# Attention in a bidirectional encoder layer: TensorE in a written order, with half of the values' projection, the queries and some of the next keys among the scores, and three steps from scores to transposes

## The chip, the core and the metric

The kernel runs on one core of one Trainium2 chip. The core has five engines, each with a queue of its own: TensorE (PE; its weight loads are listed as PEld), VectorE (DVE), ScalarE (ACT), GpSimd (POOL) and SyncE (SP), which issues most transfers. An engine takes its instructions in the order in which the built program has them, and semaphores make one wait for another. The metric is the device time of one execution in microseconds (us), lower is better; runs are compared on the same chip. The runs of the kernel before took 1503.9, 1504.07 and 1504.43 us.

## What is computed

One encoder layer on 1024 tokens and 16 meta tokens, width 1024: a combined projection, a neighbourhood attention, a gated recurrence in both directions, a gated sum of the two, an output projection and a feed-forward part, in float32. The change lies in the attention alone. The tokens are a grid of 16 rows by 64 columns; a token sees a window of 8 rows by 16 columns, and the meta tokens:

```python
# q,k,v: (B, N_META+T, H, dh), 8 heads of 64
s_win = einsum('brchd,brjwhd->bhrcjw', qg, k_blk) * scale
s_win = where(in_win, s_win + bias, -1e30)
s_meta = einsum('brchd,bmhd->bhrcm', qg, km) * scale
p = softmax(concatenate([s_win, s_meta]))
o_grid = einsum('bhrcjw,brjwhd->brchd', p_win, v_blk) + einsum('bhrcm,bmhd->brchd', p_meta, vm)
```

## The kernel before

Every float32 product is made from three matmuls of a split: each operand is a high part, which ACT casts (`hi`), and a low part, which DVE subtracts (`lo`); `mm3` (lines 122 to 124) does high by high, high by low and low by high. Below, a block is one call of `mm3`: three matmuls of the same width.

The attention runs in four pairs of heads (`NPAIR`, index `p`). A pair has three projections of 128 columns of weights over the tokens in `aT`: queries (`C_QN`, 16 blocks of 512 columns in two banks `mm`), keys (`C_KN`) and values (`C_VN`), each in three pieces of 8 blocks: 256 columns, 272 (the last 16 are the meta tokens) and 512. `proj_steps` makes them and, when it starts, splits the next weights (`load_block`: the cast L112 or L115 and the subtraction L113 or L116; those of queries, which are scaled, are L115 and L116). The order of weights is queries, keys, values, next queries.

The results go from the banks into tiles: queries into `QX` (a high half and a low half for each head of the pair), keys into `KS` (high) and `KL` (low), values into `vT`, which PE transposes (`vpt`, L831) and ACT and DVE split into `V`. There is one buffer of each, so the next pair's keys may be written when this pair's scores are done. `V` block 8 holds the meta values; it comes from the copy L825 of the 272 piece.

Then come 16 steps, one for each head `i` of the pair and strip `s` of 8 columns, in groups of four strips. `scores(s, i)` does two matmuls of 432 columns (288 at the grid's two edges) into one of two banks `s` (L848, L849); DVE adds mask and bias and takes the minimum (L854), ACT the exponential and its sum (L856), DVE the reciprocal and the scaling (L857, L858) into `pr`. `values(s, i)` transposes `pr` in three or four pieces into one of two banks `t` (`ppt`, L869, L871); ACT casts them into `PH` (L880), DVE subtracts into `PL` (L881), both named `PT` in the profile. After a group's fourth strip, the same function does the 12 matmuls with `V` into the bank `pov` (L885 to L894); DVE copies their low half (L896, `low`) and adds it into the pair's output `OT` (L898), which POOL writes out. A step's transposes stand two steps behind its scores:

```python
            for st in steps:
                pend.append((*st, *scores(*st)))
                if len(pend) > 2:
                    values(*pend.pop(0))
            for st in pend:
                values(*st)
```

Beside this, SP loads each pair's mask (`NB`) and bias, which POOL subtracts (L784), and POOL makes sums of `aT` for a later stage (`block_sums`, L189, L193).

What sets the order: inside `tc.manual_schedule(engines=...)`, the engines named run their instructions as the code is written. The context `in_order` names PE, ACT and DVE and is closed (`in_order.close()`) when the first pair's keys are done. From there a scheduler orders every engine when the program is built, from what depends on what and its own estimate of when it will be ready. It lays the next pair's projections, which the code has after the steps, between the steps; in the last pair it lays products of the next stage there (gates, L928 to L930).

Of the kernel before, what the change touches and what calls it, by code (L numbers as in the profile page):

```python
# [18 lines left out]
P = 128  # L19
# [3 lines left out]
TH = 512  # L23
# [25 lines left out]
def layer(ctx: ExitStack, tc: tile.TileContext, x, meta, w_in, w_na, w_hg, w_o, w_up, w_dn,  # L49
# [685 lines left out]
    def first_query():  # L735

        hi, lo = block_of(C_QN)
        early[C_KN] = block_of(C_KN)
        for h in range(2):
            ps = bank("mm", "mm").rearrange("p a b -> p (a b)")  # L740
            for k in range(KC):
                mm3(ps, hi[:, k], lo[:, k], *(t[:, k, :TH] for t in aT[h]), k == 0, k == KC - 1)
            yield ps
# [3 lines left out]
    query_ps = list(first_query())  # L747
# [9 lines left out]
    with (tc.tile_pool(name="npr", bufs=1, side="right", reuse_waits="tile") as npr,  # L757
# [17 lines left out]

        for p in range(NPAIR):
# [10 lines left out]
            def ev_q(ps, t0, n):  # L787
                for i in range(2):
                    act.copy(strips(QX[i], 64 * i, t0, n), grid(ps, 64 * i))
                for i in range(2):  # L790
                    b = 64 * i
                    dve.tensor_tensor(strips(QX[i], 64 - b, t0, n), grid(ps, b),
                                      strips(QX[i], b, t0, n).bitcast(F32), op=ALU.subtract)
            if p == 0:
                for h in range(2):
                    ev_q(query_ps[h], h * TH, TH)
            else:
                proj(C_QN + p * P, ev_q)

            def ev_k(ps, t0, n):  # L800
                for i in range(2):
                    act.copy(strips(KS[i], 64 * i, t0, n), grid(ps, 64 * i))
                for i in range(2):
                    b = 64 * i
                    dve.tensor_tensor(strips(KL[i], b, t0, n), grid(ps, b),
                                      strips(KS[i], b, t0, n).bitcast(F32), op=ALU.subtract)
                    act.copy(strips(KS[i], 64 - b, t0, n), strips(KS[i], b, t0, n).bitcast(F32))

            def mev_k(ps):
                for i in range(2):  # L810
                    b = 64 * i
                    m = ps[b:b + 64].unsqueeze(1).broadcast_to([64, 8, NM])
                    hi = KS[i][b:b + 64, :, P:]
                    act.copy(hi, m)
                    act.copy(KS[i][64 - b:128 - b, :, P:], m)
                    dve.tensor_tensor(KL[i][b:b + 64, :, P:], m, hi.bitcast(F32), op=ALU.subtract)
            proj(C_KN + p * P, ev_k, mev_k)
            in_order.close()

# [6 lines left out]
            proj(C_VN + p * P, ev_vn, mev_vn)  # L826
            for b in (0, 4, 8):
# [33 lines left out]
            def values(s, i, js, pr):  # L861
# [20 lines left out]
                if e < 3:  # L882
                    return
# [12 lines left out]
                dve.tensor_copy(low, ov[64:])  # L896
# [992 lines left out]
```

## Time and profile before

| | |
|---|---|
| profiled execution | 1503.19 us, its span 1501.4 us |
| runs of the kernel | 1503.9, 1504.07, 1504.43 us |
| PE | 9200 matmuls in the trace, 1488.8 us busy |
| granted TensorE clock | 0.999 of full speed |
| attention, first scores to last products | from 354.5 us of the span to about 562 us |
| one pair, from values' transposes to the next pair's | 57.27, 56.48, 56.44 us |

The profile is one execution, recorded by the hardware's profiler. A row of the timeline has an instruction's start in us from the span's start, how long it took, engine, line, operation, output and inputs by the program's names, partitions and elements, and the count where equal ones are merged; in brackets the idle time of the engine ahead of it and what ended it. Rows of groups have the sum of busy time and the mean in ns of one. A row of windows has the stretch, its length, then for each engine in the order PE, PEld, DVE, ACT, POOL the busy us and the count of instructions, then the clock, the busy share of the transfer engines and GB/s. PE's matmuls are pipelined and their ends modelled: a 512-column matmul is shown with 0.39 us and the next starts 0.23 later. So what a matmul takes is read from starts.

### The profile page before, as it was taken

What the parts mean: (1) busy time and instruction counts of PE and PEld (TensorE: products, weight loads), DVE (VectorE), ACT (ScalarE), POOL (GpSimd) and SP (SyncE); (2) the same over time, 40 slices, a digit from 0 to 9 for tenths busy, and PEclk for the clock granted to TensorE, in tenths of its full rate; (3) what the DMA queues carried; (4) which work ended last, traced back from release to release, by engine and by line L of the source; (5) the groups of instructions that cost most, each with busy time, mean ns of one, the idle gap of its engine ahead of it and who ended that gap; (6) DMA issues with size and microseconds to landing.
All of it is one profiled execution on the core that took longest, in us unless ns stands there. A gap on an engine that the chain in (4) does not pass through costs nothing.

```text
span 1501.4 us, 23486 instructions
## 1 busy us (share of the span) xinstructions
PE 1488.8 (99%) x9200; PEld 1249.0 (83%) x9200; DVE 1045.1 (70%) x1612; ACT 669.5 (45%) x1197; POOL 366.3 (24%) x346
## 2 busy tenths in 40 slices
PE   9999999999999999999999999999999999999998
PEld 8888888888888888888888887888888888888886
DVE  7867676756696696665485479777777445877876
ACT  7232323136565576343132355555555534334444
POOL 3313131314423400110000122234444200231242
PEclk9999999999999999999999999999999999999999
DMA  4211011112313237445655125444444677563224
GB/s 171 60 29 58 29 58 29 58 51 98 109 43 95 98 116 235 147 155 176 209 169 210 43 99 175 155 155 154 154 155 155 209 259 234 189 225 115 95 83 155
DMA packets 142592, 195.61 MB, mean 130 GB/s; under 512 B 8193, under 2 KB 90369, under 8 KB 142481
## 3 DMA queue, kind: packets, MB, share of 16 engines
q1 hardware_dynamic: 133216, 172.86, 35.2%
q10 hardware_dynamic: 7088, 13.91, 2.4%
q0 software_dynamic: 2176, 7.34, 1.3%
q8 instruction: 72, 1.18, 0.3%
q14 instruction: 40, 0.32, 0.1%
HBM read 139.56 MB, written 54.53 MB: 129 GB/s over the span
## 4 chain that ended last, share of the span: by engine, by line
PE 92%; DVE 5%; ACT 2%; issue 1%; DMA 0%; POOL 0%; ACTq 0%; POOLq 0%; DVEq 0%
PE mm L122 11%; PE mm L123 11%; PE mm L124 11%; PE mm L1564 5%; PE pa L1564 5%; PE pb L928 4%; PE pb L929 4%; PE pb L930 4%; PE pc L1564 4%; PE pb L1564 4%; PE pc L929 3%; PE pc L930 3%; PE pc L928 3%; PE pa L930 2%; PE pa L929 2%; PE pa L928 2%
## 5 line engine op out<-in xcount | busy, mean ns | idle before, releaser
L122 PE MATMUL mm<-aT,hi 128*128 128x512 f32 (+2 forms) x600 | 214.5, 358 | 0.0
L124 PE MATMUL mm<-aT,lo 128*128 128x512 f32 (+2 forms) x600 | 211.7, 353 | 0.0
L123 PE MATMUL mm<-aT,hi 128*128 128x512 f32 (+2 forms) x600 | 211.0, 352 | 0.0
L97 DVE TENSOR_TENSOR dl<-ur,dh 128x1024 fp32r<-128x1024 f32 x54 | 71.1, 1316 | 87.3 <-ACT dh L96 85.4
L96 ACT CAST dh<-ur 128x1024 fp32r<-128x1024 f32 x54 | 56.9, 1054 | 166.7 <-issue 91.1
L122 PEld LDWEIGHTS mm<-aT,hi 128*128 128x128 f32 x600 | 113.3, 189 | 12.5
L124 PEld LDWEIGHTS mm<-aT,lo 128*128 128x128 f32 x600 | 113.2, 189 | 12.5
L123 PEld LDWEIGHTS mm<-aT,hi 128*128 128x128 f32 x600 | 113.4, 189 | 11.4
L1352 ACT ACTIVATE uv<-uv 128x512 f32<-128x512 f32 x48 | 30.4, 633 | 79.3 <-DVE uv L1460 52.8
L112 ACT CAST hi<-raw 128x1024 fp32r<-128x1024 f32 x26 | 27.3, 1050 | 64.5 <-PE mm L123 62.1
L854 DVE CUSTOM_DVE_ANT_0 pr<-nsc,NB 128x432 f32<-128x432 f32 (+1 forms) x64 | 35.2, 558 | 30.0 <-issue 21.6
L1655 POOL TENSOR_TENSOR w<-w,tt 128x512 f32<-128x512 f32 x16 | 23.4, 1460 | 133.1 <-DVE tt L1654 112.3
L113 DVE TENSOR_TENSOR lo<-raw,hi 128x1024 fp32r<-128x1024 f32 x26 | 38.4, 1476 | 18.0 <-ACT hi L112 14.0
L303 POOL TENSOR_TENSOR Y<-X,TN 128x512 f32<-128x512 f32 x20 | 31.1, 1556 | 80.3 <-DVE X L300 80.3
L122 PE MATMUL mm<-wh,mT 128*128 128x512 f32 x128 | 50.2, 392 | 0.0
L123 PE MATMUL mm<-wl,mT 128*128 128x512 f32 x128 | 50.1, 391 | 0.0
L124 PE MATMUL mm<-o,lo 128*128 128x512 f32 x128 | 49.9, 390 | 0.1
L124 PE MATMUL mm<-wh,mT 128*128 128x512 f32 x128 | 49.9, 390 | 0.0
L123 PE MATMUL mm<-o,hi 128*128 128x512 f32 x128 | 49.8, 389 | 0.0
L122 PE MATMUL mm<-o,hi 128*128 128x512 f32 x128 | 49.8, 389 | 0.0
L1564 PE MATMUL mm<-dl,dh 128*128 128x512 f32 x124 | 48.6, 392 | 0.3 <-DVE dl L97 0.2
L1564 PE MATMUL mm<-dh,dl 128*128 128x512 f32 x124 | 48.3, 390 | 0.0
(459 smaller groups left out, 4439.3 us busy)
## 6 DMA issues: line engine op xcount, KB each, us to landing
raw<-in_w_in SPq DMA_DIRECT2D x56, 512.0 KB, 4.0
ur<-usp SPq DMA_DIRECT2D x54, 512.0 KB, 3.6
raw<-in_w_up SPq DMA_DIRECT2D x16, 1024.0 KB, 6.1
usp<-us SPq DMA_DIRECT2D x60, 256.0 KB, 2.3
sg<-gsp SPq DMA_DIRECT2D x16, 512.0 KB, 5.0
w<-in_w_dn SPq DMA_DIRECT2D x16, 512.0 KB, 4.8
usp<-uv SPq DMA_DIRECT2D x30, 256.0 KB, 2.4
gsp<-gv ACTq DMA_DIRECT2D x24, 256.0 KB, 2.4
```

The costliest lines, as they stand in the source:

```text
L96: act.copy(hi, src)
L97: dve.tensor_tensor(lo, src, hi.bitcast(F32), op=ALU.subtract)
L113: dve.tensor_tensor(lo[:, :kc], raw[:, :kc], hi[:, :kc].bitcast(F32), op=ALU.subtract)
L122: pe.matmul(ps, lh, rh, start=first, stop=False)
L123: pe.matmul(ps, lh, rl, start=False, stop=False)
L124: pe.matmul(ps, ll, rh, start=False, stop=last)
L303: pool.tensor_tensor(fap(Y, h, mid3), fap(X, h, mid3), fap(TT, 0, [[4, g], [n + 3, 2], [0, h]]), op=ALU.mult)
L854: dve.tensor_tensor_reduce(out=pr[:, :w], in0=sc[:, :w], in1=NB[:, i, o:o + w], scale=1.0, scalar=3.0e38, op0=ALU.add, op1=ALU.min, accum_ ...
L928: pe.matmul(ps, lhs[0][:, c], rhs[0][:, k], start=first and k == 0, stop=False, skip_group_check=True)
L929: pe.matmul(ps, lhs[0][:, c], rhs[1][:, k], start=False, stop=False, skip_group_check=True)
L930: pe.matmul(ps, lhs[1][:, c], rhs[0][:, k], start=False, stop=k == 3, skip_group_check=True)
L1564: pe.matmul(ps, a[n == 2][:, q, j * P:(j + 1) * P], b[n == 1][:, q], start=first and n == 0, stop=last and n == 2, skip_group_check=True)
```

## The change

- `in_order` is closed after a pair's keys as before, but opened again for PE alone. So PE runs as written until the seventh step of the last pair; ACT and DVE are left to the scheduler.
- The values' first 12 blocks (`VAHEAD`) are written ahead of the scores. The other 12, the transposes of the values, the next pair's queries and the first of its keys are one stream (`fills`), from which `columns` takes blocks into two gaps of each step, by a table of columns (`GAPS`).
- A step's transposes stand three steps behind its scores, and a group's products (`products`, cut out of `values`) in the step after.
- The last three transposes and the last products (`tail`) are written into the next pair's keys. The next pair's queries are evicted after steps 13 and 16, and evictions of keys are held back until the scores are done.
- The copy into `low` goes from DVE to ACT.

The lines of the kernel after are some 50 to 70 further down: L869 is L919, L848 is L898, L831 is L859, L825 is L854, L822 is L851, L856 is L906, L880 is L930, L885 is L937.

First, PE in the second pair, around its first scores and the transposes of its values. `nsc` are scores, `mm` with `aT_89` and `aT_90` the values' 512 piece (with `aT_87` and `aT_88` their smaller pieces or the next queries), `vpt` the values' transposes. Before, from the last matmul ahead of the values' first eight transposes to that of the meta values:

```order
L124 MATMUL mm<-aT_87,lo 128x512
L831 MATMUL vpt<-ident,vT 128x128 x8
L122 MATMUL mm<-aT_87,hi 128x512
L848 MATMUL nsc<-KS_4068,QX_4066 128x288
L849 MATMUL nsc<-KL_4070,QX_4066 128x288
L123 MATMUL mm<-aT_88,hi 128x512
L124 MATMUL mm<-aT_87,lo 128x512
L122 MATMUL mm<-aT_87,hi 128x512
L848 MATMUL nsc<-KS_4068,QX_4066 128x432
L849 MATMUL nsc<-KL_4070,QX_4066 128x432
L123 MATMUL mm<-aT_88,hi 128x512
L831 MATMUL vpt<-ident,vT 128x128
```

After, from the second scores:

```order
L898 MATMUL nsc<-KS_4067,QX_4065 128x432
L899 MATMUL nsc<-KL_4069,QX_4065 128x432
L122 MATMUL mm<-aT_87,hi 128x272
L123 MATMUL mm<-aT_88,hi 128x272
L124 MATMUL mm<-aT_87,lo 128x272
L122 MATMUL mm<-aT_87,hi 128x272
L123 MATMUL mm<-aT_88,hi 128x272
L124 MATMUL mm<-aT_87,lo 128x272
L859 MATMUL vpt<-ident,vT 128x128
L122 MATMUL mm<-aT_89,hi 128x512
L123 MATMUL mm<-aT_90,hi 128x512
L124 MATMUL mm<-aT_89,lo 128x512
```

All of the values' blocks stood ahead of the scores, and so of these rows; the matmuls between the scores are the next pair's queries. Now the scores lie among the values' blocks, and the transpose of the meta values comes right behind the blocks of 272 columns, the last of which makes them.

Second, ACT over the same stretch, up to the transposes' casts. `pr,sm` are exponentials, `hi` the cast of the next projection's weights, `vT` copies of the values (16 for the meta values, 64x8x64 for the 512 piece), `Vn` casts of the transposed values. Before:

```order
L822 COPY vT<-mm 64x8x32 x2
L825 COPY vT<-mm 128x16
L822 COPY vT<-mm 64x8x32 x2
L112 CAST hi<-raw 128x1024
L822 COPY vT<-mm 64x8x64 x2
L856 ACTIVATE pr,sm<-pr,mn 128x288
L856 ACTIVATE pr,sm<-pr,mn 128x432
L833 CAST Vn<-vpt 128x8x64 x2
L856 ACTIVATE pr,sm<-pr,mn 128x432 x2
L833 CAST Vn<-vpt 128x2x64
L880 CAST PT_5025<-ppt 128x3x128
```

After:

```order
L906 ACTIVATE pr,sm<-pr,mn 128x288
L906 ACTIVATE pr,sm<-pr,mn 128x432
L854 COPY vT<-mm 128x16
L851 COPY vT<-mm 64x8x32 x2
L861 CAST Vn<-vpt 128x2x64
L906 ACTIVATE pr,sm<-pr,mn 128x432 x2
L930 CAST PT_5013<-ppt 128x3x128
L930 CAST PT_5013<-ppt 128x4x128
L906 ACTIVATE pr,sm<-pr,mn 128x288
L112 CAST hi<-raw 128x1024
L906 ACTIVATE pr,sm<-pr,mn 128x432
L851 COPY vT<-mm 64x8x64 x2
```

The copies into `vT` stood ahead of the first exponential. Now that of the meta values stands behind two exponentials, and those of the 512 piece behind a cast of weights and one exponential more. (In the first pair the orders are others: there `vT` of 16 stands ahead of the second exponential, and the 512 piece's copies ahead of the cast.)

Third, PE where the other values are turned, from the second of two query blocks behind the values' last block:

```order
L122 MATMUL mm<-aT_87,hi 128x512
L123 MATMUL mm<-aT_88,hi 128x512
L124 MATMUL mm<-aT_87,lo 128x512
L898 MATMUL nsc<-KS_4068,QX_4066 128x432
L899 MATMUL nsc<-KL_4070,QX_4066 128x432
L859 MATMUL vpt<-ident,vT 128x128 x4
L919 MATMUL ppt<-ident,pr 128x128 x3
L921 MATMUL ppt<-ident,pr 128x128
L122 MATMUL mm<-aT_87,hi 128x512
```

Before, the eight transposes stood ahead of the fifth scores, as the first rows show; now four stand behind the seventh scores, with a step's transposes of `pr` right behind them.

The core of the diff:

```diff
+    query_ps = []
+    def query_steps(p, tile):
+        hi, lo = block_of(C_QN + p * P)
+        early[C_KN + p * P] = block_of(C_KN + p * P)
         for h in range(2):
-            ps = bank("mm", "mm").rearrange("p a b -> p (a b)")
+            ps = tile()
             for k in range(KC):
                 mm3(ps, hi[:, k], lo[:, k], *(t[:, k, :TH] for t in aT[h]), k == 0, k == KC - 1)
-            yield ps
+                if k == KC - 1:
+                    query_ps.append(ps)
+                yield TH
...
+        def ev_q(h, i):
+            b = 64 * i
+            ps = query_ps[h]
+            act.copy(strips(QX[i], b, h * TH, TH), grid(ps, b))
+            dve.tensor_tensor(strips(QX[i], 64 - b, h * TH, TH), grid(ps, b),
+                              strips(QX[i], b, h * TH, TH).bitcast(F32), op=ALU.subtract)
...
+        scoring, held = [], []
+        def ev_k_held(ps, t0, n):
+            if scoring:
+                held.append(lambda: ev_k(ps, t0, n))
+            else:
+                ev_k(ps, t0, n)
+        keys = [proj_steps(C_KN + p * P, ev_k_held, mev_k) for p in range(NPAIR)]
+        def columns(fill, n):
+            ahead_by[0] -= n
+            while ahead_by[0] < 0:
+                ahead_by[0] += next(fill, -ahead_by[0])
+        ahead_by = [0]
+        GAPS = ([(520, 520)] * 5 + [(512, 682), (512, 682), (1024, 0), (300, 300), (300, 300), (300, 700), (700, 0),
+                (300, 300), (300, 300), (400, 900), (900, 0)])
+        VAHEAD = KC + 4
...
+            query_ps.clear()
+            fill = keys[p]
+            for f in tail:
+                columns(fill, 5 * 256)
+                f()
+            list(fill)
             in_order.close()
+            in_order.enter_context(tc.manual_schedule(engines={pe.engine}))
...
+                return m * P // 3
+            def fills(values, queries):
+                for k in range(2 * KC - VAHEAD):
+                    yield next(values)
+                yield turn_values(8)
+                yield from values
+                for b in (0, 4):
+                    for _ in range(2):
+                        yield next(queries, 0)
+                    yield turn_values(b)
+                yield from queries
+            def queries_and_keys():
+                if p + 1 < NPAIR:
+                    yield from query_steps(p + 1, mm_tile)
+                    for n in keys[p + 1]:
+                        yield n
+            value_steps = proj_steps(C_VN + p * P, ev_vn, mev_vn)
+            for _ in range(VAHEAD):
+                next(value_steps)
...
+            def products(s, i):
+                g = s // 4
+                PH, PL = po[i]
...
-                dve.tensor_copy(low, ov[64:])
+                act.copy(low, ov[64:])
...
-            pend = []
-            for st in steps:
+            fill = fills(value_steps, queries_and_keys())
+            pend, due, tail = [], [], []
+            scoring.append(p)
+            for n, st in enumerate(steps):
                 pend.append((*st, *scores(*st)))
-                if len(pend) > 2:
-                    values(*pend.pop(0))
-            for st in pend:
-                values(*st)
-            pool.dma_start(osp[1][p], OT)
+                if p + 1 < NPAIR and n in (12, 15):
+                    for q in ((0, 0),) if n == 12 else ((0, 1), (1, 0), (1, 1)):
+                        ev_q(*q)
+                if p == NPAIR - 1 and n == 6:
+                    in_order.close()
+                    list(fill)
+                columns(fill, GAPS[n][0])
+                while due:
+                    products(*due.pop())
+                if len(pend) > 3:
+                    s, i, *q = pend.pop(0)
+                    values(s, i, *q)
+                    if s % 4 == 3:
+                        due.append((s, i))
+                columns(fill, GAPS[n][1])
+            scoring.clear()
+            while held:
+                held.pop(0)()
+            def last(s, i, *q):
+                return lambda: values(s, i, *q)
+            tail += [last(*q) for q in pend]
+            tail += [lambda dst=osp[1][p]: (products(7, 1), pool.dma_start(dst, OT))]
+            if p == NPAIR - 1:
+                for f in tail:
+                    f()
```

More of the change, by code (lines that the diff above doesn't have):

```diff
@@ L733, in layer @@
         prev = cur
-    def first_query():
-        hi, lo = block_of(C_QN)
-        early[C_KN] = block_of(C_KN)
+    query_ps = []
+    def query_steps(p, tile):
+        hi, lo = block_of(C_QN + p * P)
+        early[C_KN + p * P] = block_of(C_KN + p * P)
         for h in range(2):
-            ps = bank("mm", "mm").rearrange("p a b -> p (a b)")
+            ps = tile()
             for k in range(KC):
                 mm3(ps, hi[:, k], lo[:, k], *(t[:, k, :TH] for t in aT[h]), k == 0, k == KC - 1)
-            yield ps
+                if k == KC - 1:
+                    query_ps.append(ps)
+                yield TH
     in_order = ExitStack()
     in_order.enter_context(tc.manual_schedule(engines={e.engine for e in (pe, act, dve)}))
-    query_ps = list(first_query())
+    list(query_steps(0, lambda: bank("mm", "mm").rearrange("p a b -> p (a b)")))
     list(prev)
@@ L774, in grid, with ev_k, mev_k @@
             return ps[p0:p0 + 64].rearrange("p (r s c) -> p s r c", s=8, c=8)
+        def ev_q(h, i):
[4 more added lines that the diff above has]
+                              strips(QX[i], b, h * TH, TH).bitcast(F32), op=ALU.subtract)
+        def ev_k(ps, t0, n):
+            for i in range(2):
+                act.copy(strips(KS[i], 64 * i, t0, n), grid(ps, 64 * i))
+            for i in range(2):
+                b = 64 * i
+                dve.tensor_tensor(strips(KL[i], b, t0, n), grid(ps, b),
+                                  strips(KS[i], b, t0, n).bitcast(F32), op=ALU.subtract)
+                act.copy(strips(KS[i], 64 - b, t0, n), strips(KS[i], b, t0, n).bitcast(F32))
+        def mev_k(ps):
+            for i in range(2):
+                b = 64 * i
+                m = ps[b:b + 64].unsqueeze(1).broadcast_to([64, 8, NM])
+                hi = KS[i][b:b + 64, :, P:]
+                act.copy(hi, m)
+                act.copy(KS[i][64 - b:128 - b, :, P:], m)
+                dve.tensor_tensor(KL[i][b:b + 64, :, P:], m, hi.bitcast(F32), op=ALU.subtract)
+        scoring, held = [], []
[13 more added lines that the diff above has]
+        VAHEAD = KC + 4
+        tail = []
         for p in range(NPAIR):
@@ L785, in layer @@
                                        op=ALU.subtract)
[L787 to L793, printed above, removed]
-            if p == 0:
[L795 to L817, printed above, removed]
+            if p == 0:
+                for q in ((0, 0), (0, 1), (1, 0), (1, 1)):
+                    ev_q(*q)
[5 more added lines that the diff above has]
+            list(fill)
             in_order.close()
+            in_order.enter_context(tc.manual_schedule(engines={pe.engine}))
             def ev_vn(ps, t0, n):
@@ L825, in mev_vn, with turn_values @@
                 act.copy(vT[:, 8, P - NM:], ps)
-            proj(C_VN + p * P, ev_vn, mev_vn)
-            for b in (0, 4, 8):
+            def turn_values(b):
                 pt = bank("t", "vpt")
```

3 lines of the change are left out of this document (1 added, 2 removed).

## The prediction

> **What bounds the kernel now.** I read the page first: the span, the busy shares, then the chain of work that ended last.
>
> ```profile
> span 1501.4 us, 23486 instructions
> ...
> PE 1488.8 (99%) x9200; PEld 1249.0 (83%) x9200; DVE 1045.1 (70%) x1612; ACT 669.5 (45%) x1197; POOL 366.3 (24%) x346
> ...
> PE 92%; DVE 5%; ACT 2%; issue 1%; DMA 0%; POOL 0%; ACTq 0%; POOLq 0%; DVEq 0%
> ```
>
> TensorE (PE) is busy all the time and carries 92% of the chain, so the kernel gets shorter only where PE does something in less time. No part of the change removes a matmul: the orders of before and after list the same PE instructions, as often each. What can go is time that PE loses between matmuls, and a busy share does not show it, since a matmul's end is modelled. So I count from start to start. The change touches the attention over four pairs of heads; I cut it where the eight transposes of the values (`vpt`, L831) start, and take the stretches.
>
> ```profile
> 356.82:414.09 57.27, 56.33 (x342) 47.92 (x342) 43.09 (x109) 35.89 (x85) 20.48 (x21) 1.00 0.31 98
> 414.09:470.57 56.48, 56.02 (x343) 48.19 (x343) 43.79 (x109) 34.60 (x84) 20.84 (x20) 1.00 0.26 82
> 470.57:527.01 56.44, 55.96 (x342) 48.25 (x342) 43.65 (x109) 34.59 (x84) 18.23 (x18) 1.00 0.23 75
> 527.01:562.90 35.89, 35.86 (x211) 29.87 (x211) 33.90 (x93) 27.74 (x65) 0.00 (x0) 1.00 0.39 120
> ```
>
> The first number behind the colon is the stretch's length. What its work takes when nothing waits comes from rows of one timeline of PE, each from its start to the start of the next row.
>
> ```profile
> 440.38 0.49 PE L869 MATMUL ppt<-ident,pr 128*128 128x128 f32 x3
> ...
> 440.82 0.49 PE L869 MATMUL ppt<-ident,pr 128*128 128x128 f32 x3
> ...
> 444.00 0.28 PE L124 MATMUL mm<-aT,lo 128*128 128x256 f32 x1
> 444.12 0.28 PE L122 MATMUL mm<-aT,hi 128*128 128x256 f32 x1
> 444.75 0.41 PE L869 MATMUL ppt<-ident,pr 128*128 128x128 f32 x2 [0.35 <-DVE pr L858]
> ...
> 463.46 0.39 PE L122 MATMUL mm<-aT,hi 128*128 128x512 f32 x1
> 463.69 0.40 PE L123 MATMUL mm<-aT,hi 128*128 128x512 f32 x1
> ...
> 468.36 0.29 PE L849 MATMUL nsc<-KL,QX 128*128 128x288 f32 x1
> 468.49 0.36 PE L848 MATMUL nsc<-KS,QX 128*128 128x432 f32 x1
> ...
> 468.89 0.40 PE L122 MATMUL mm<-aT,hi 128*128 128x512 f32 x1
> ```
>
> A 256-column matmul takes 0.12 us (444.00 to 444.12), a 512 one 0.227, four transposes 0.44 or 0.109 each (440.38 to 440.82), a 288 one 0.13, two of 432 0.40. For 272, 384 and 128 columns I take 0.125, 0.175 and 0.06, between these by columns. A full stretch has 104 matmuls of 512 columns, 64 of 256, 48 of 272, 24 of 432, 16 of 384, 8 of 288, 8 of 128 and 69 transposes: 53.9 us. The three full stretches therefore lose 3.4, 2.6 and 2.6 us. The last, by its own counts 34.5 us, loses 1.4. **All that the change can win is these 10 us.** The rows show one such loss: the matmul at 444.12 should be over by 444.24, and the transposes start at 444.75, half a microsecond late, held by the softmax of VectorE (DVE). Part of the loss no order takes away: a switch between transposes and matmuls costs about 0.01 us, 19 times a pair, and 0.3 I leave for small things. I take 0.5 us a pair as a floor that stays.
>
> Why the losses arise is seen in two stretches of one pair, the scores and the projections.
>
> ```profile
> 414.10:446.10 32.00, 31.54 (x197) 26.60 (x197) 30.81 (x89) 23.14 (x57) 4.06 (x5) 1.00 0.16 50
> 446.10:468.20 22.10, 22.10 (x137) 19.91 (x136) 11.19 (x16) 9.14 (x23) 16.23 (x16) 1.00 0.43 138
> ```
>
> Among the scores DVE is busy 30.8 of 32.0 us, among the projections 11.2 of 22.1. While scores run, DVE is nearly as full as PE.
>
> **The change, part by part.** (1) The products of a group of four strips come one step after their last transposes, behind at least two matmul blocks. The casts that they waited for have then landed, and the 0.1 to 0.2 us by which each came late goes. (2) A pair's transposes lie three steps behind its scores rather than two. A step of PE is about 2 us (two score matmuls 0.40, four transposes 0.44, two projection blocks of three matmuls 1.36), so the softmax has some 6 us. Waits such as the one at 444.75 go, and what is late next is below. (3) The copy of the low halves moves from DVE to ScalarE (ACT): 16 instructions each way, 4 a pair. DVE is rid of 2.8 us a pair by the row of L896 below, ACT pays the like with its 0.58 us copy, and it has room, since the pair's ACT sum is 34.6 of 56.5 us. (4) The values' projection is cut: 12 of its 24 blocks run before the first score and 12 among scores. Queries and a few keys of the next pair follow there, so the softmax has more matmuls beside it. None of these matmuls is added. (5) On GpSimd (POOL) the write of a pair's output now stands ahead of the next pair's bias work. That work then starts about when the keys end, and takes 2.5 us for the first head:
>
> ```profile
> 443.43 2.48 POOL L784 TENSOR_TENSOR NB<-NB,bs 128x384 f32<-128x384 f32 x3 [27.87 <-DMA NB<-in_wmask]
> ```
>
> Its first reader comes with the first scores, some 5 us after the keys' end (worked out below). The tail of matmuls hides it; without that cover it would cost up to 2.5 us a pair. (6) Queries' banks are now freed in steps 13 and 16, the keys' second piece needs one 5 us later by PE's rows, and each eviction is 0.6 us on ACT (the two of L789 below): hidden.
>
> But PE now keeps its written order, and so every matmul behind a late one waits too. I went along PE's order and asked, at each wait, where ACT and DVE stand in theirs. The rows for this:
>
> ```profile
> 430.20 0.59 DVE L854 CUSTOM_DVE_ANT_0 pr<-nsc,NB 128x432 f32<-128x432 f32 x1
> 430.72 0.07 DVE L854 DVE_READ_ACCUMULATOR2_ANT mn<- 128x1 f32 x1
> ...
> 468.79 0.46 DVE L854 CUSTOM_DVE_ANT_0 pr<-nsc,NB 128x288 f32<-128x288 f32 x1 [6.68 <-issue]
> ```
> ```profile
> 430.89 0.66 ACT L856 ACTIVATE pr<-pr,mn 128x432 f32<-128x432 f32 x1 [0.44 <-DVE rc L857]
> 431.45 0.19 ACT L856 ACTIVATION_READ_ACCUMULATOR pr<-pr,mn 128x1 f32 x1
> ...
> 442.03 1.06 ACT L112 CAST hi<-raw 128x1024 fp32r<-128x1024 f32 x1
> 442.98 1.18 ACT L789 CAST QX<-mm 64x512 fp32r<-64x512 f32 x2
> ...
> 462.96 0.17 ACT L825 COPY vT<-mm 128x16 f32<-128x16 f32 x1 [1.91 <-PE mm L124]
> ...
> 469.28 1.18 ACT L822 COPY vT<-mm 64x512 f32<-64x512 f32 x2
> ```
>
> *The meta values, pairs 2 to 4.* PE does the second scores, two blocks of 272 columns, then the one transpose of the meta values, which needs ACT's copy `vT` (0.17 us). In ACT's order that copy stands behind the second exponential. From the start of the second scores: the second matmul starts at 0.20 and is out at 0.56; DVE takes it 0.14 later (468.36 plus 0.29, to 468.79), at 0.70; the exponential starts 0.69 behind DVE's start (430.20 to 430.89), at 1.39; it holds ACT 0.65; the copy ends at 2.21. PE is there at 0.40 plus 0.75, 1.15. **Wait: 1.1 us.** Behind it stand the blocks of the values' last piece and the third scores, for which DVE then has nothing to do. In the first pair the copy stands ahead of that exponential and there is no wait.
>
> *The other values, pairs 2 and 3.* From the end of the values' last matmul ACT does the next keys' split (0.95, from 442.03 to the next start), an exponential (0.65), two copies (1.18): the values are there at 2.8. PE reaches their transposes after four transposes, two query blocks and two scores, 0.45 plus 1.36 plus 0.40, at 2.2. **Wait: 0.6 us.** The next transposes need the bank of the last but one, which ACT casts only behind those copies (0.5 more, to 3.3) and DVE then subtracts from (0.60), to 4.0. PE is there at 2.8 plus 0.45, 3.25. **Wait: 0.7 us.** In the first pair the copies come ahead of the split, so only the bank is late, by 0.9. In the fourth a scheduler orders PE from the seventh score on and puts ten 512 matmuls in; I leave 0.4 for this.
>
> *The keys' end.* Twelve value blocks, 8 of 0.36 and 4 of 0.375 us, lie between a pair's last key matmul and its first scores: 4.4 us, where the whole projection of 11.3 lay before.
>
> ```profile
> 401.45 1.23 DVE L116 SCALAR_TENSOR_TENSOR lo<-raw,hi 128x1024 fp32r<-128x1024 f32 x1 [2.81 <-ACT hi L115]
> ...
> 456.65 0.39 PE L124 MATMUL mm<-aT,lo 128*128 128x512 f32 x1
> ...
> 456.85 1.06 ACT L115 ACTIVATE hi<-raw 128x1024 fp32r<-128x1024 f32 x1 [1.86 <-PE mm L123]
> 457.94 1.19 ACT L802 CAST KS<-mm 64x512 fp32r<-64x512 f32 x2
> ...
> 457.94 2.75 DVE L116 SCALAR_TENSOR_TENSOR lo<-raw,hi 128x1024 fp32r<-128x1024 f32 x1 [2.92 <-ACT hi L115]
> 460.72 1.39 DVE L805 TENSOR_TENSOR KL<-mm,KS 64x512 fp32r<-64x512 f32 x2
> ```
>
> From the last key matmul at 456.65 to the keys' low halves at 462.11 is 5.46 us, because the next query weights' split (L116) stands ahead of them on ACT and DVE. PE will want them at 0.23 plus 4.38 plus 0.13, 4.74. With the split at 2.75 us the wait is 0.7, with 1.23 us, as in the pair before, there is none. I take 0.4 in pairs 2 and 3, and keep 0 and 0.7.
>
> Why L116 differs, the Trainium skill explains in "SBUF — State Buffer", section "Who interferes with whom": a DVE instruction with two SBUF inputs and a GpSimd one that reads SBUF block each other for a whole instruction, whoever is first. That agrees with 2.75 beside 1.23 here, and since (5) puts POOL's subtractions just there, by that rule both pairs would pay the full 0.7 and the sum would be 0.6 higher.
>
> **Sum.** Pair 1: 0.5 floor plus 0.9 is 1.4, against 3.4: 2.0 less. Pairs 2 and 3: 0.5, 1.1, 0.6, 0.7 and 0.4 are 3.3, against 2.6: 0.7 more each. Pair 4: 0.5, 1.1 and 0.4 are 2.0, against 1.4: 0.6 more. Together 0.0. The profiled execution took 1503.19 us (a span of 1501.4), 0.9 below the median of 1504.07; set on the median, the forecast is **1504.1 us**.
>
> **The rivals.** *The old waits go and the new ones don't come* (chance 0.20). If ACT reaches the `vT` copies in time, all pairs are like pair 1 as forecast: 1.4 against 3.4, 2.6, 2.6 and 1.4, which is 4.4 less: 1499.7. For it speaks that two of the three waits hang on some 0.6 us; against it that the 1.1 us is a chain of three engines in a fixed order. With the floor alone it would be 8.0 less, 1496.1.
>
> *DVE becomes the bound in the second half of the scores* (chance 0.14), the case on the other side. Steps 9 to 16 have fewer matmuls.
>
> ```profile
> L881 DVE TENSOR_TENSOR PT<-ppt,PT 128x512 fp32r<-128x512 f32 x12 | 8.1, 677 | 0.1
> L854 DVE CUSTOM_DVE_ANT_0 pr<-nsc,NB 128x432 f32<-128x432 f32 x12 | 7.1, 592 | 0.0
> L858 DVE TENSOR_SCALAR pr<-pr,rc 128x432 f32<-128x432 f32 x12 | 5.2, 436 | 0.1
> L857 DVE RECIPROCAL rc<-sm 128x1 f32<-128x1 f32 x16 | 2.4, 153 | 0.4 <-ACT pr L856 0.2
> L896 DVE COPY low<-pov 64x512 f32<-64x512 f32 x4 | 2.8, 690 | 0.4 <-PE pov L894 0.4
> ```
>
> PE has there 6300 columns three times (8.4 us), scores 2.9, transposes 3.4, three groups of products 5.2 by the matmuls above: about 20 with the switches. A step of DVE is, by these means, 0.59, 0.44, 0.68 and 0.15, and 0.07 for the read of the minimum: 1.93, or 15.4 for eight, plus three additions and four subtractions of the queries at the 0.69 of L896, which has their size (4.8), and one weight split (1.2): 21.4. Counted from start to start the first is 0.52 rather than 0.59 (430.20 to 430.72), and with all shortened like it the sum is 19. By the longer sum DVE is 1.4 us behind, which three steps of lead (5 us), less the softmax's own 2.5, still cover. It decides once DVE is more than 2.5 us behind, as when the split takes L116's 2.75 (1.5 more) and each of some 45 instructions starts 0.02 later (0.9): 3.8 behind, so 1.3 us in each of pairs 1 to 3: 1508.0.
>
> *Nothing gets there* (chance 0.05): PE is not freed, because what the order moves is moved again by ACT's and DVE's scheduler; the losses keep their 10 us and the time is that of before, 1504.1 as well. The rows of the order speak against it.
>
> **How the numbers follow.** The forecast has 0.61. Its own errors are the 0 to 0.7 at the keys' ends (0.8 us down, 0.6 up), and a third of the other waits (6.3 us in pairs 2 to 4, so 2.1): about 1501.2 to 1507.0. The range takes in the first rival's 1499.7 and the second's 1508.0: **1499.5 to 1508.0**. Within 0.2% (3 us, about what a measurement of this kernel can tell from no change) lie the third case, and most of the forecast: 0.64. Faster gets the first rival and a little of the forecast, 0.21; slower the second rival and as much, 0.15.
>
> **What would show it.** In PE's timeline of the changed kernel, the transpose of the meta values of pairs 2 to 4 should start about 1.1 us late, with ACT's exponential just ahead of `vT`; the next value transposes 0.6 and the transposes behind them 0.7; the first scores' second matmul up to 0.7, ended by the keys' low halves. Waits like that of 444.75 should be gone. A stretch from values to values should be near 55.3 us in pair 1 and 57.2 in pairs 2 and 3. It is wrong if transposes late in a pair wait for DVE's `pr` or `PT`, or if pairs 2 and 3 fall below 56 us.

## The result, and the profile after

The changed kernel takes **1512.67 us** (median of 6 runs, 1511.17 to 1513.44) against 1504.43 (6 runs, 1503.9 to 1504.84) for the kernel before on the same chip: ratio **1.0054, 95% interval 1.0043 to 1.0065**. It is 8.2 us slower; forecast was 1504.1, with a range up to 1508.0.

The page of the changed kernel, with the lines that answer to those of before:

```profile
span 1511.1 us, 23461 instructions
...
PE 1490.3 (99%) x9200; PEld 1251.9 (83%) x9200; DVE 1038.0 (69%) x1596; ACT 681.7 (45%) x1213; POOL 362.9 (24%) x346
```

PE's busy time has grown by 1.5 us (1488.8 to 1490.3), the span by 9.7. So most of the loss lies between PE's matmuls, and it has to be counted from start to start again. I cut both kernels where a pair's first score starts; from there to the next pair's first score lies one full pair, 53.9 us of work by the prediction's count. Stretches of the kernel before, the last one to the last product:

```profile
354.49:411.74 57.25, 56.31 (x343) 47.89 (x341) 43.07 (x108) 35.88 (x85) 21.77 (x22) 1.00 0.33 104
411.74:468.23 56.49, 56.03 (x342) 48.20 (x341) 43.81 (x108) 34.61 (x84) 20.99 (x20) 1.00 0.26 82
468.23:524.68 56.45, 55.97 (x343) 48.25 (x341) 43.66 (x108) 34.60 (x84) 18.74 (x19) 1.00 0.23 75
524.68:562.89 38.21, 38.18 (x222) 31.53 (x220) 35.66 (x97) 30.00 (x68) 0.00 (x0) 1.00 0.36 112
```

The same of the changed kernel:

```profile
348.69:405.79 57.10, 55.45 (x343) 48.32 (x342) 41.52 (x105) 38.73 (x88) 25.14 (x26) 1.00 0.26 85
405.79:464.01 58.22, 55.46 (x343) 48.68 (x342) 41.58 (x104) 37.71 (x87) 19.14 (x20) 1.00 0.25 80
464.01:522.23 58.22, 55.43 (x344) 48.69 (x343) 41.11 (x105) 37.71 (x87) 17.30 (x19) 1.00 0.24 78
522.23:564.50 42.27, 41.34 (x239) 34.05 (x238) 33.96 (x93) 31.22 (x70) 1.70 (x3) 1.00 0.28 87
```

Less 53.9 the full pairs lost 3.3, 2.6 and 2.5 us and now lose **3.2, 4.3 and 4.3**; the last, by its own matmuls, 1.8 and now **3.2**. That is 10.3 and 15.0. So 4.8 of the 9.7 us between the two spans are in the pairs. The next largest part lies behind them, in the gates:

```profile
574.28 0.39 PE L1002 MATMUL mm<-aT,lo 128*128 128x512 f32 x1
576.76 0.50 PE L1000 MATMUL mm<-aT,hi 128*128 128x512 f32 x1 [2.09 <-ACT go L1021]
...
577.61 0.63 PE L1000 MATMUL mm<-aT,hi 128*128 128x512 f32 x1
578.03 0.63 PE L1001 MATMUL mm<-aT,hi 128*128 128x512 f32 x1
```

The matmul at 574.28 should be followed at 574.51; the next starts at 576.76, held by ScalarE's sigmoid (L1021). And from 577.61 each matmul takes 0.427 us (to 578.03) rather than 0.227. Two windows of it, the gap and the slow matmuls (PEclk is the number behind POOL's):

```profile
574.51:576.76 2.25, 0.16 (x2) 0.01 (x1) 1.01 (x2) 2.17 (x3) 0.00 (x0) 1.00 1.13 370
577.40:581.00 3.60, 3.60 (x11) 2.82 (x10) 2.04 (x2) 2.29 (x3) 0.00 (x0) 0.53 0.94 353
```

The granted clock is 0.53 in the second. Gap and slow matmuls cost 4.0 us together, where the kernel before lost nothing in the 45 us behind its last product. 4.8 and 4.0 are 8.8.

Ahead of the first score another 1.1 us had gathered (and the stages further behind give some 0.3 back). Of these 0.6 arise where the two programs are the same, between one execution and another; in the other profiles it is 0.1 to 0.6. The other 0.5 are of the change, and stand in the profile of every kernel with it:

```profile
335.14 0.28 PE L124 MATMUL mm<-aT,lo 128*128 128x256 f32 x1
335.77 0.36 PE L122 MATMUL mm<-aT,hi 128*128 128x272 f32 x1 [0.34 <-DVE QX L784]
```

The first keys' second piece should start at 335.26 and waits for the bank of the first pair's queries. The new `ev_q` takes a cast and a subtraction in turn, and ScalarE's second cast starts at 334.31, behind VectorE's first subtraction (333.59); before, the first two casts stood together at 325.63, and no matmul waited here.

Inside the pairs the view of PE's waits names these, from 345 to 606 us (total, times, longest):

```profile
PE ppt L919 <- DVE PT L931: 2.8, 3, 1.3
PE vpt L859 <- DVE rc L907: 2.8, 3, 0.9
PE mm L1000 <- ACT go L1021: 2.1, 1, 2.1
PE pov L937 <- ACT PT L930: 1.6, 3, 0.7
PE vpt L859 <- ACT vT L851: 0.8, 2, 0.4
```

before, the same view has two:

```profile
PE ppt L869 <- DVE pr L858: 1.1, 3, 0.4
PE ppt L869 <- DVE Vn L834: 0.5, 1, 0.5
```

So the old wait for the softmax (`pr`) is gone, as forecast, and the waits for the values are there, as forecast. Pair 2 of the changed kernel, in PE's timeline:

```profile
407.82 0.29 PE L124 MATMUL mm<-aT,lo 128*128 128x272 f32 x1
409.04 0.33 PE L859 MATMUL vpt<-ident,vT 128*128 128x128 f32 x1 [0.93 <-DVE rc L907]
...
419.02 0.36 PE L899 MATMUL nsc<-KL,QX 128*128 128x432 f32 x1
419.77 0.66 PE L859 MATMUL vpt<-ident,vT 128*128 128x128 f32 x4 [0.39 <-ACT vT L851]
421.19 0.52 PE L919 MATMUL ppt<-ident,pr 128*128 128x128 f32 x3 [0.77 <-DVE PT L931]
...
453.92 0.39 PE L124 MATMUL mm<-aT,lo 128*128 128x512 f32 x1
454.98 0.50 PE L937 MATMUL pov<-PT,Vn 128*128 128x512 f32 x1 [0.67 <-ACT PT L930]
```

and ScalarE ahead of the first and the last of these:

```profile
408.05 0.66 ACT L906 ACTIVATE pr<-pr,mn 128x432 f32<-128x432 f32 x1 [0.56 <-DVE mn L904]
...
408.82 0.17 ACT L854 COPY vT<-mm 128x16 f32<-128x16 f32 x1
...
453.01 0.76 ACT L789 CAST KS<-mm 64x256 fp32r<-64x256 f32 x2
...
454.66 0.27 ACT L930 CAST PT<-ppt 128x128 fp32r<-128x128 f32 x1
```

From 407.82 plus 0.125 to 409.04 is 1.1 us: the meta values' transpose, just behind the end of `vT` (408.99), which stands behind the second exponential. (The view put this wait down to VectorE's `rc`, which ended at the same moment; the exponential's row settles it.) 419.02 plus 0.197 to 419.77 is 0.55 (0.57 in pair 3), 419.77 plus 0.48 (four transposes, and a switch) to 421.19 is 0.93. The prediction's sum has nothing for the last: the pair's final products, among the next pair's keys, 0.83 late (453.92 plus 0.227 to 454.98), for a cast of their last transposes that stands behind the keys' evictions.

### The profile page after: what moved, and what is told of

The parts are those of the page before. It is cut to its first block, busy times and chain, and to the rows that moved or that the text cites. A ratio compares the mean times of both kernels' runs of the same rounds, so it can differ in the third digit from the quotient of the medians.

```text
span 1511.1 us, 23461 instructions
## 1 busy us (share of the span) xinstructions
PE 1490.3 (99%) x9200; PEld 1251.9 (83%) x9200; DVE 1038.0 (69%) x1596; ACT 681.7 (45%) x1213; POOL 362.9 (24%) x346
## 4 chain that ended last, share of the span: by engine, by line
PE 91%; DVE 4%; ACT 3%; DMA 1%; issue 1%; SPq 0%; POOL 0%; ACTq 0%; POOLq 0%; DVEq 0%
PE mm L122 11%; PE mm L124 10%; PE mm L123 10%; PE mm L1636 5%; PE pa L1636 5%; PE pb L1000 4%; PE pb L1001 4%; PE pb L1002 4%; PE pc L1636 4%; PE pb L1636 4%; PE pc L1001 3%; PE pc L1002 3%; PE pc L1000 3%; PE pa L1001 2%; PE pa L1000 2%; PE pa L1002 2%
## 5 line engine op out<-in xcount | busy, mean ns | idle before, releaser
L906 ACT ACTIVATE pr<-pr,mn 128x432 f32<-128x432 f32 (+1 forms) x64 | 40.1, 627 | 21.2 <-DVE mn L904 20.5
```

What stands on the lines that cost most here:

```text
L906: act.activation(pr[:, :w], pr[:, :w], AF.Exp, bias=mn, scale=-1.0, accum_out=sm)
```

## The experiments

Losses in the texts below are counted as above. They stand together here; "behind" is the 45 us behind the last product. Each ratio is to the kernel before as it ran beside that one on the same chip (1503.87 to 1504.43 us). The losses are those of one profiled execution each.

| kernel | us | ratio to before, 95% interval | pairs 1, 2, 3, 4 | sum | behind |
|---|---|---|---|---|---|
| before | 1504.43 | | 3.3, 2.6, 2.5, 1.8 | 10.3 | 0.0 |
| changed | 1512.67 | 1.0054, 1.0043 to 1.0065 | 3.2, 4.3, 4.3, 3.2 | 15.0 | 4.0 |
| last pair as before | 1513.04 | 1.0051, 1.0037 to 1.0065 | 3.2, 4.4, 4.3, 2.2 | 14.0 | 5.9 |
| meta behind values | 1509.88 | 1.0038, 1.0025 to 1.0051 | 5.4, 3.0, 4.0, 2.3 | 14.7 | 3.9 |
| values later | 1510.90 | 1.0043, 1.0030 to 1.0056 | 3.1, 4.3, 4.3, 3.2 | 14.9 | 2.9 |
| products later | 1509.99 | 1.0036, 1.0024 to 1.0049 | 2.6, 3.4, 3.3, 3.2 | 12.6 | 4.2 |
| gates' order | 1508.99 | 1.0029, 1.0018 to 1.0041 | 3.1, 4.3, 4.3, 3.2 | 14.9 | 0.7 |
| products and gates | 1506.67 | 1.0016, 1.0007 to 1.0025 | 2.6, 3.4, 3.3, 3.3 | 12.5 | 0.9 |
| the same, meta two blocks later | 1503.95 | 1.0002, 0.9993 to 1.0011 | 3.0, 2.2, 2.2, 2.1 | 9.5 | 0.4 |
| lead of two steps | 1514.74 | 1.0067, 1.0055 to 1.0080 | 5.7, 3.0, 4.2, 2.3 | 15.2 | 6.0 |
| scheduler | 1503.24 | 0.9992, 0.9983 to 1.0001 | 2.6, 2.1, 2.0, 2.0 | 8.6 | 0.9 |
| scheduler, products | 1499.97 | 0.9974, 0.9964 to 0.9984 | 1.9, 1.1, 1.0, 2.0 | 6.0 | 0.6 |
| scheduler, products and gates | 1500.42 | 0.9976, 0.9967 to 0.9986 | 2.0, 1.1, 1.2, 2.0 | 6.3 | 1.0 |
| the same, low copy on VectorE | 1500.16 | 0.9975, 0.9965 to 0.9985 | 2.0, 1.1, 1.0, 2.3 | 6.4 | 0.2 |

**Who orders TensorE?** The line that puts TensorE into a written order for the attention is left out.

```diff
             in_order.close()
-            in_order.enter_context(tc.manual_schedule(engines={pe.engine}))
```

> The code of the change, but TensorE is not in a written order during the attention: the scheduler places its matmuls, as it does for the other engines. Theory A (the late starts in pairs 1 to 3 are the price of a fixed order, in which everything behind a late matmul waits): the attention's pairs lose about what they lost before, 10 instead of 15 us, and the gates' idle of 4.0 stays: 1507.7. Theory B (the late starts come from where the values, their transposes and the products now lie, and whoever orders TensorE meets them): within 1 us of 1512.7.

1503.24 us: 9.4 less than the changed kernel, no slower than before. Theory A for the pairs (15.0 to 8.6 us); its other half, that the gates' 4.0 stay, did not hold: they shrank to 0.9, and why they did is not shown. PE's waits are now:

```profile
PE pov L936 <- ACT PT L929: 1.6, 3, 0.7
PE ppt L918 <- DVE PT L930: 0.6, 1, 0.6
PE mm L999 <- ACT go L1020: 0.6, 1, 0.6
PE vpt L858 <- ACT vT L850: 0.2, 1, 0.2
```

The scheduler moved little. In pair 2 it put the transpose of the meta values one block of 512 columns and one score matmul later, and two matmuls of a block between a score and the first four values' transposes, and four more ahead of the transposes behind these. The first of it:

```profile
408.05 0.36 PE L897 MATMUL nsc<-KS,QX 128*128 128x432 f32 x1
408.45 0.33 PE L858 MATMUL vpt<-ident,vT 128*128 128x128 f32 x1
```

408.05 plus 0.197 to 408.45 is 0.2 us where the written order waited 1.1, and the matmuls that stood behind the wait went ahead of it.

**The transpose of the meta values.** First behind all values' blocks, then (with two other edits, below) two blocks later only.

```diff
-                yield turn_values(8)
                 yield from values
+                yield turn_values(8)
```

> In pairs 1 to 4 the one transpose of the meta values stands behind the last value block instead of behind the second scores. Theory A (each late start of TensorE in its written order is a loss of its own): the three waits of 1.1 us of pairs 2 to 4 go, 3.3 us: 1509.4. Theory B (VectorE and ScalarE pace the scores, so a wait that is taken away comes back at the next one): the time stays, 1512.7, and the waits at the value transposes behind it grow by as much.

1509.88 us, at theory A's number, but the trace says otherwise. The three waits of 1.1 went, and pairs 2 to 4 lose 1.3, 0.3 and 1.0 us less; pair 1, which never had this wait, loses 2.2 more. There a step's transposes wait for a bank that VectorE's subtraction is to free; that the nine value transposes, now closer together, crowd the two banks is an inference:

```profile
359.37 0.40 PE L124 MATMUL mm<-aT,lo 128*128 128x512 f32 x1
361.93 0.87 PE L919 MATMUL ppt<-ident,pr 128*128 128x128 f32 x3 [2.17 <-DVE PT L931]
```

That bank's wait is 2.33 us (359.60 to 361.93) instead of 1.47, 0.9 more, and the matmuls behind it run at half clock for a while (last section). The sum of the pairs falls by 0.4 us alone. The profiled execution is the slowest of the five (1511.9, the others from 1507.89), 0.9 below that of the changed kernel; the 2.8 us between the medians are not seen in it.

```diff
+                for k in range(2):
+                    yield next(values)
                 yield turn_values(8)
```

> The written order on TensorE, with the later products and t2 behind the sigmoid (1506.7 without more), and the transpose of the meta values two blocks of the values' last piece (1.36 us) later, ahead of the third scores. Theory A (the wait of 1.1 us is the distance to ScalarE's copy and nothing is late in its place): 3.3 us less: 1503.4. Theory B (in a written order the next late instruction takes the wait over): 1506.7, within 1 us, and the waits at the other values' transposes are longer.

1503.95 us, 2.7 less than the 1506.67 without it: theory A. This kernel's waits in the attention:

```profile
PE ppt L921 <- DVE PT L933: 2.9, 3, 1.3
PE vpt L859 <- ACT vT L851: 1.4, 3, 0.6
```

No meta value waits, and the other values' waits in pairs 2 and 3 are as long as they were, 0.56. Only in pair 1, which had no such wait to lose, the wait for `vT` grows from 0.25 to 0.81, and the pair loses 0.4 more, about what 2.7 lacks of 3.3. So in pairs 2 to 4 the wait was a distance of two blocks and not a bound of ScalarE or VectorE.

**The other values.**

```diff
-                for b in (0, 4):
-                    for _ in range(2):
+                for b, m in ((0, 3), (4, 2)):
+                    for _ in range(m):
                         yield next(queries, 0)
```

> One more query block before the first group of value transposes in pairs 1 to 3 (both groups come about 0.7 us of TensorE's work later). Theory A (their wait is only that ScalarE's copies of the values come 0.57 us late, and the bank behind them): the 0.57 goes in pairs 2 and 3 and 0.25 in pair 1, and 0.7 of the bank's wait (1.47 in pair 1, 0.93 in pairs 2 and 3) each: 3.5 us, 1509.2. Theory B (the bank is what is short, and the transposes of the scores wait for it wherever the values' come): the 0.57 and 0.25 go, the rest stays, 1.4 us: 1511.3.

1510.90 us, near theory B's number, but not by its mechanism: the pairs' sum is the same within 0.2, which neither theory said. The values' transposes no longer wait for `vT`, but 0.86 us for the bank, and the first products 0.57 us for the second group's values; 0.56 and 0.93 became 0.86 and 0.57. The gain lies outside the pairs (1.1 us of it behind them, where the sigmoid's wait is 1.1 instead of 2.1 and the clock stays full behind it), so this wait is moved, not removed.

**A pair's last products.**

```diff
-            for f in tail:
-                columns(fill, 5 * 256)
+            for j, f in enumerate(tail):
+                columns(fill, (9 if j == 3 else 5) * 256)
```

> Among the next pair's keys four more blocks of keys (0.48 us each 1280 columns more or less: 1024 columns thrice, 1.4 us) stand before the last products of a pair. Theory A (these products wait for ScalarE's last cast of their transposes, 0.42 us in pair 1 and 0.83 in pairs 2 and 3): the waits go, 2.1 us: 1510.6. Theory B (the wait is made up later, since the next pair's first scores wait for the keys anyway): the time stays, 1512.7.

1509.99 us, and the pairs lose 2.5 us less: theory A. The next pair's first scores did not give it back. With the scheduler and this edit:

> The changed code with TensorE left to the scheduler in the attention, and four more blocks of keys ahead of a pair's last products. Theory A (the late products are a loss beside that of the written order): 2.1 us less than with the scheduler alone (1503.2): 1501.1, faster than before the change. Theory B (what the scheduler wins it wins by filling just these waits): 1503.2.

**1499.97 us, ratio 0.9974 (0.9964 to 0.9984)**: faster than both kernels, theory A (3.3 us less than the scheduler alone, 2.1 expected). One wait over 0.5 us is left in the attention, that of pair 1's bank:

```profile
PE ppt L918 <- DVE PT L930: 0.6, 1, 0.6
```

**The gates' start.** The gates' code is the same in both kernels; it has ScalarE, VectorE and SyncE in a written order. Two theories of the 4.0 us: values pushed gate blocks back, or ScalarE's order holds the sigmoid. The first was tried by giving the last pair its old place for values.

```diff
-                for k in range(2 * KC - VAHEAD):
+                for k in range(2 * KC - VAHEAD if p + 1 < NPAIR else 0):
...
-            for _ in range(VAHEAD):
+            for _ in range(VAHEAD if p + 1 < NPAIR else 3 * KC):
...
-                if p == NPAIR - 1 and n == 6:
+                if p == NPAIR - 1 and n == 0:
```

> The last pair alone goes back to its old place for values: all 24 value blocks and the nine value transposes before its scores, and from its first score on TensorE is left to the scheduler, so gate blocks stand among the scores from the start. Pairs 1 to 3 stay as changed. Theory A (the idle 2.25 us at 574 of the changed kernel, and the nine matmuls behind it at about half the clock, 1.75 us, come from gate blocks pushed behind the attention by the value blocks): both go, 4.0 us, and with them this pair's meta-values wait of 1.1: 1507.6. Theory B (the idle belongs to the later end of the attention and the table load of ScalarE, wherever the values are): the idle and the slow stretch stay, only the 1.1 goes: 1511.6.

1513.04 us: theory B, and its number missed by 1.4. The last pair loses about 1 us less, and the idle grows by as much and more:

```profile
PE mm L1000 <- ACT go L1021: 4.0, 1, 4.0
```

TensorE got to the gap 1.5 us earlier (572.78 instead of 574.28), and the sigmoid came no earlier (576.56 and 576.11). What the sigmoid waits for is seen on ScalarE of the changed kernel, and on the queue of SyncE:

```profile
571.08 0.62 ACT L96 CAST aT<-gv 128x512 fp32r<-128x512 f32 x1 [1.23 <-DMA gv<-tsp_t]
572.79 2.01 ACT L96 CAST aT<-gv 128x512 fp32r<-128x512 f32 x3 [1.08 <-DMA gv<-tsp_t]
574.81 1.28 ACT L1021 ACT_TABLE_LOAD   x1
576.11 0.60 ACT L1021 ACTIVATE go<-mm 128x512 f32<-128x512 f32 x1
...
564.81 2.98 SPq L1082 DMA_DIRECT2D gv<-tsp_t  x4
```

The four loads of t2, an operand of the gates (`gv`), go out from 564.81, 0.3 us behind the last product (564.50), and land some 6 us later; their four splits, a table load of 1.28 us and the sigmoid follow in ScalarE's written order. Before, these loads began at 556.36, 6.5 us ahead of the last product (562.89):

```profile
556.36 2.09 SPq L1010 DMA_DIRECT2D gv<-tsp_t  x4
```

So t2 went behind the sigmoid:

```diff
         pss = [first_products_1(b) for b in pair]
-        for _ in ops["t2"]:
-            pass
         last_pair = first_weights_of((6, 7), gp, wp)
         for b, ps, c in zip(pair, pss, last_pair):
             first_products_2(b, ps)
             split_block(c)
+        for _ in ops["t2"]:
+            pass
```

> In the gates' written order on ScalarE, VectorE and SyncE the four loads and splits of the operand t2 stand behind the second products of the blocks 2 and 3, with their sigmoid, instead of ahead of them; all else is as changed. Theory A (TensorE idles 2.25 us at 574 because ScalarE must split t2 before it may free a bank by the sigmoid, and t2's loads go out only when the attention is nearly over; the half clock behind it is a consequence of the idling): both go, 4.0 us: 1508.7. Theory B (the banks are late for another reason, such as the table load, or the wait returns at the first product that needs t2): the time stays above 1511.5.

1508.99 us, 3.7 less: theory A. Here the sigmoid waits for TensorE and not the other way round, and the matmuls behind it run at full clock:

```profile
571.64 0.60 ACT L1021 ACTIVATE go<-mm 128x512 f32<-128x512 f32 x1 [0.83 <-PE mm L1002]
...
PE mm L1000 <- ACT go L1021: 0.2, 1, 0.2
```

Both edits together:

> Both at once: four more blocks of keys before a pair's last products, and t2 behind the sigmoid of blocks 2 and 3. Theory A (the two losses are apart): 2.7 and 4.0 us less than the changed kernel: 1506.0. Theory B (what the attention gains, the gates' start loses, since the loads that hold the gates come no earlier): 1508 or more.

1506.67 us, 6.0 less: theory A, the losses are apart. With the scheduler there is little left for it to win:

> The same with t2's loads and splits behind the sigmoid of blocks 2 and 3. Theory A (of the gates' idling 0.75 us are left when the scheduler orders TensorE, and they go): 1500.4. Theory B (the gates' start is paced by the loads alone and stays): 1501.1.

1500.42 us, ratio 0.9976 (0.9967 to 0.9986). The number is theory A's, but the version without this edit had 1499.97, so it brings nothing, as theory B said. Without the edit the wait had already shrunk to 0.2 us; with it, another matmul starts 0.9 us late for a sigmoid, at 580.12. That the loads alone pace this start is not shown.

**The third step.**

```diff
-                if len(pend) > 3:
+                if len(pend) > 2:
```

(and the products held where they are).

> The transposes of a strip come two steps behind its scores again instead of three; the products stay in the steps in which they are now. Theory A (the third step is what takes the softmax's waits away: from the ninth score on a pair loses 0.3 us now, and lost 1.7 before the change): about 1.3 us more in each of pairs 1 to 3, 3.9: 1516.6. Theory B (the many matmuls that now lie among the scores take the waits away, and the third step is idle cover): 1512.7, within 1 us.

1514.74 us, between the theories. The old wait is back, `ppt` for `pr` 1.1 us in two places (1.1 in three before the change, none with three steps), so the third step does take it away. But the products' wait of 1.6 is gone, the meta values wait less, pair 1 pays more for its bank, and the pairs' sum stays at 15.2. The 2.1 us lie in the gates' start (6.0 instead of 4.0): TensorE waits 0.9 longer there, and the half clock behind it lasts until 583.3 us rather than 580.6. So in this order the third step moves waits and saves nothing in the pairs. Whether two or three steps are better with the scheduler was not tried.

**The copy of the low halves**, on VectorE again, in the version of 1500.42 us:

```diff
-                act.copy(low, ov[64:])
+                dve.tensor_copy(low, ov[64:])
```

> The third version of these four (scheduler, later products, t2 behind the sigmoid) with the copy of the low halves back on VectorE, 16 instructions of 0.69 us. Theory A (with the third step VectorE has room, 0.7 to 3 us idle in each part of a pair's scores, so the copy can stand on either engine): within 0.7 us of that version. Theory B (VectorE is so full in the second half of the scores, 1.5 us idle of 9.2 there, that the copy makes transposes late): 2 to 3 us slower.

1500.16 us, ratio 0.9975 (0.9965 to 0.9985). Theory A: with TensorE left to the scheduler this part of the change is worth nothing.

## Why the prediction was wrong

By its own terms, with what was measured:

- *The old waits go* (1, 2, 4). Right: no softmax wait from the ninth score on; brought back by two steps of lead.
- *The low copy* (3), *the bias work and the queries' banks* (5, 6). Put at nothing; the copy measured at nothing (with the scheduler), and no wait for the others is in the view from 345 us on. The order that (5) gave did not come: GpSimd's bias work for pair 2 is done at 397.0, and the write of pair 1's output follows at 410.99. And (6) thought of the later pairs' queries alone; those of the first pair cost 0.5 us.
- *The meta values*, 1.1 us in pairs 2 to 4, none in pair 1. Measured 1.10 each time, and taken away by a distance of two blocks. Right, and right to the size.
- *The other values*, 0.6 and a bank of 0.7 in pairs 2 and 3: 0.56 and 0.93. In pair 1 0.9 for the bank: 1.5, and 0.25 for the values. 1.2 us too little in these three.
- *The keys' end*, 0.4 in pairs 2 and 3: none. The split L116 took 1.23 us ahead of pair 2, where no GpSimd sum ran as it started, and 2.04 ahead of pair 3, from 460.70, while a GpSimd sum (L189) ran until 461.65. The keys' low halves were done at 464.06, and their first reader came at 464.14, without a wait. By the Trainium skill's rule on blocking ("SBUF — State Buffer", section "Who interferes with whom") the prediction had both pairs pay 0.7; the 2.04 agrees with the rule, and here it cost TensorE nothing.
- *A pair's last products*. The sentence of (1) that the casts "have then landed" failed in this place: 0.42, 0.83 and 0.83 us. It holds for the products among the scores and not for the last ones, whose casts stand behind ScalarE's evictions of the next keys. 2.1 us, shown by taking it away.
- *The floor*, 0.5 us a pair. What no named wait explains is 0.9 to 1.1 in pairs 1 to 3 and 2.1 in pair 4, where the scheduler mixes gates in; some 2.5 us too little, with the 0.4 left for pair 4's values set against it. With the scheduler and the later products, where pairs 2 and 3 have no wait over 0.2, they still lose 1.1 and 1.0. The 0.5 was worked out from the gaps' cause (a switch, 0.01) and not from what the stretches of before left after their own gaps.
- *What comes behind the attention* was in no term. The sum ended with the last product, and took for granted that the stage behind starts as before. It costs 4.0 us, the largest single error; the new order of t2 took 3.3 of it away. TensorE came to a bank that ScalarE was to free, while ScalarE stood in a written order behind loads that went out only as the attention ended. The price of a written order was asked for on TensorE only, although the gates have one on three other engines.

10.0 forecast, plus 4.0, 2.1, 2.5 and 1.2, less 0.8 at the keys, is 19.0, the 15.0 of the pairs and the 4.0 behind them. **What failed is the list of places, and not the mechanism**: a late start in a fixed order costs its length, as forecast, and there were more of them, the largest outside the stretch that was summed. The slower rival had the right sign for the wrong reason. It named pairs 1 to 3, and there VectorE was not the bound: from the ninth to the thirteenth score of pair 2 it is busy 7.7 us of 9.2. In pair 4, which it did not name, VectorE is as full as that rival feared:

```profile
426.62:435.80 9.18, 9.18 (x57) 8.00 (x56) 7.66 (x22) 6.07 (x15) 0.00 (x0) 1.00 0.02 4
539.33:547.87 8.54, 8.54 (x54) 7.11 (x54) 8.50 (x27) 6.40 (x16) 0.00 (x0) 1.00 0.19 56
```

TensorE loses 0.2 us in the first stretch and 0.7 in the second, a part of pair 4's 2.1; whether VectorE is the cause was not tried.

Not settled: why gates' blocks come so late in the last pair in the scheduler's order, what else pair 4 loses, and the medians of the second experiment.

## What to carry to other kernels

An order written by hand turns each estimate that is off by a microsecond into a microsecond lost, where a scheduler puts two blocks in between; here the new placement, with one distance mended and TensorE left to the scheduler, was worth 4 us, and the fixed order cost 9 (1512.67 to 1503.24). With three places mended by hand the fixed order came to 1503.95, the time of before. When a stage is moved or made denser, follow the loads and banks of the next stage through every queue with an order of its own, until they meet the old times again. And take a floor of small losses from what is left over in a measured stretch, not from a list of causes.

## What the hardware showed

TensorE's granted clock fell to about one half behind gaps of some 2 us. Windows of the kernel with the meta values behind all values (the matmuls behind 2.17 us of waiting), and of the one with the values later (behind 1.58 us), the clock being the number behind POOL's:

```profile
362.60:365.10 2.50, 2.50 (x10) 2.10 (x10) 1.52 (x2) 0.59 (x1) 0.58 (x1) 0.52 0.30 92
```
```profile
364.30:368.00 3.70, 3.70 (x23) 3.17 (x22) 3.52 (x10) 2.42 (x6) 0.00 (x0) 1.00 0.48 140
```

0.52 in the one, 1.00 in the other. Among the waits of TensorE from the attention on, in all the profiles here, those of up to 1.58 us left the clock alone (1.11, 1.21, 1.31 and 1.58 among them); the seven longer ones, of 1.85, 1.99, 2.09, 2.17, 2.30, 2.99 and 4.04 us, were each followed by 2.4 us or more at 0.50 to 0.54. Between 1.58 and 1.85 nothing was measured. The Trainium skill ("TensorE: Matmul & The Clock Gate", section "What's actually happening") puts the half clock behind at least one idle window of about 3.4 us, in windows that run freely; here a wait of 1.85 us was enough, and the measurement decides. The gap of 2.25 us in the changed kernel thus cost 4.0.
